# A two-layer hybrid block on one core: the high parts of the weight tiles are cast on GpSimd instead of ScalarE during attention

## The chip, the cores and the metric

The kernel runs on one core of one Trainium2 chip. The metric is the time of one execution on the device in microseconds, as the median of several runs. The engines are TensorE (PE in the rows, PEld its weight loads), VectorE (DVE), ScalarE (ACT), GpSimd (POOL) and SyncE (SP), which here issues the DMAs.

## The reference

Two layers work on 512 latent tokens and 256 context tokens of width 1024. In each, a modulated RMS norm feeds one wide projection, whose columns go to three mixers (windowed attention with a sink and rotary positions, multi-scale pooling, a Fourier mix) and three gates. The branches are gated, summed and projected; a gated MLP with a depthwise convolution follows.

```python
h = modulate(rms_norm(x, norm_mix[l]), sh1, sc1)
k, v, q, u, f, gt = jnp.split(h @ w_in[l], IN_SPLITS, axis=-1)
q = apply_rope(q.reshape(B, T, N_Q_HEADS, HEAD_DIM), cos, sin)
o = latent_attention(q, k, v, kc, vc, attn_sink[l])
y = (g_a * (o_attn @ w_br_attn)
     + g_p * (multiscale_pool(pool_in, pool_w, pool_scale) @ w_br_pool)
     + g_f * (fourier_mix(four_in) @ w_br_four))
x = x + g1 * (y @ w_out)
x = x + g2 * conv_ffn(hf, w_up[l], conv_w[l], w_down[l])
```

In layer 0 the context tokens go the same way (768 columns in all); in layer 1 only their keys and values are needed, and 512 columns run through the rest.

## The kernel before

Activations lie with channels on the partitions and tokens along the columns. The large products are made in float32r with every operand split into a high part (the value rounded to float32r) and a low part (the rest): a product is three matmuls, high by high, high by low and low by high (`mmk`, line 373). The split of a weight tile is made on the chip, in `halves` (line 345): a cast of the raw tile on ScalarE writes the high part `whi` (line 353), and VectorE subtracts it from the raw tile to get the low part `wlo` (line 354). A tile is 128 partitions by 1024 columns. There are three buffers each for the raw tile, for `whi` and for `wlo`.

Tiles are drawn in a planned order (`_plan`, line 70). `weights` (line 362) hands out the tile at the head, after `ahead` (line 357) has loaded and split the one behind it; so each draw splits the next tile. The raw tiles are loaded by DMAs from SyncE's queue (`raw`, line 340).

The attention phase (`attention`, line 753) lays two kinds of work side by side on TensorE. One is the attention proper, in units of one head pair and one block of 128 queries: `scores` makes the scores in PSUM (lines 688 to 699; there is one such PSUM buffer), VectorE takes the maximum (line 704) and the bias (line 707), ScalarE the exponentials (lines 713 and 715), VectorE the sums and the scaling (lines 716 to 720); `turn_p` transposes the result on TensorE (line 736) and copies it out (line 737), one unit later; `pv` multiplies by the values (line 747), two units later. The other kind stands in the list `BESIDE`: four query tiles (`q_steps`, line 637) and eight gates of the Fourier branch (`gate_steps`, line 598), cut into steps that are put between the units. A query tile draws one `w_in` tile, and a gate draws one, with a `w_brf` tile before every fourth gate. Behind a query tile's matmuls stands its rope: a copy out of PSUM (line 628), a shuffle on VectorE (line 631), one product on VectorE (line 632) and one on GpSimd (line 633), their sum (line 634), the cast and the subtraction into the query tiles (lines 647 and 648). A gate ends with tanh on ScalarE (line 607), a product on VectorE (line 613) and a sum on GpSimd (line 615).

The order on TensorE in this phase is the program's own (`manual_schedule`, line 892). On the other engines a planner orders the instructions when the program is built, by its own estimate of when each one becomes ready; so an instruction that goes to another engine, or takes another time there, may also change the order of its neighbours. Each engine then works through its queue in order.

Of the kernel before, what the change touches and what calls it, by code (L numbers as in the profile page):

```python
# [69 lines left out]
def _plan(l):  # L70
    tiles = lambda *ms: [("w_in", l, m) for m in ms]

    def gates(name, first, n):
        for m in range(8):
            if m % n == 0:
                yield (name, l, m // n)
            yield ("w_in", l, first + m)

    yield from tiles(0, 1, 4, 5, 2, 3) if l else tiles(3)
    yield from gates("w_brp", 10, 4)  # L80
    if l == 0:
        yield from tiles(4, 5)
    gf = gates("w_brf", 18, 4)
    for kind, j in BESIDE:
        if kind == "q":
            yield ("w_in", l, 6 + j)
        else:
            yield from (next(gf) for _ in range(1 + (j % 4 == 0)))
    for m in range(8):
        if m % 2 == 0:  # L90
            yield ("w_bra", l, m // 2)
        yield ("w_in", l, 26 + m)
    for ms in (range(8), range(KEEP[0])):
        yield from (("w_out", l, m) for m in ms)
    for c, (j0, n) in enumerate(FF_CHUNKS):
        for j in range(j0, j0 + n):
            yield from (("w_up", l, j), ("w_up", l, NFF + j))
        if 0 < c < len(FF_CHUNKS) - 1:
            yield from (("w_dn4", l, c - 1, i) for i in range(4))
    for ms in (range(8), range(0 if l else KEEP[0])):  # L100
        yield from (("w_dn6", l, m) for m in ms)


class Lazy:
    def __init__(self, make, n):
        self.make, self.t = make, [None] * n
# [33 lines left out]
class Kern:  # L140
    def __init__(self, ctx, tc, a):
        self.tc, self.nc, self.a = tc, tc.nc, a
        e = ctx.enter_context
        self.cp = e(tc.tile_pool(name="cp", bufs=1))
        self.wr = e(tc.tile_pool(name="wr", bufs=3))
        self.wp = e(tc.tile_pool(name="wp", bufs=3))
        self.sm = e(tc.tile_pool(name="sm", bufs=4))
        self.dp = e(tc.tile_pool(name="dp", bufs=1, space=bass.MemoryType.DRAM))
        self.sp = e(tc.tile_pool(name="sp", bufs=NSLOT))
        self.mm_pool = e(tc.tile_pool(name="mp", bufs=NP, space=bass.MemoryType.PSUM))  # L150
        self.cv_pool = e(tc.tile_pool(name="cv", bufs=2))
        self.tg_pool = e(tc.tile_pool(name="tg", bufs=1))
        self.scopes, self.nph, self.turn, self.cturn = [], 0, 0, 0
        self.fill = iter(())
        self.plan = deque(k for l in range(NL) for k in _plan(l))
        self.ready = deque()
        self.pend = iter(())
# [187 lines left out]
    def halves(self, raw, eng=None, stay=False):  # L345
        nc = self.nc
        n = raw.shape[-1]
        if stay:
            hi, lo = self.slot(), self.slot()
        else:  # L350
            hi = self.wp.tile([P, 1024], F32R, tag="whi", name="whi")[:, 0:n]
            lo = self.wp.tile([P, 1024], F32R, tag="wlo", name="wlo")[:, 0:n]
        self.cpy = nc.scalar.copy(hi, raw)  # L353
        (eng or nc.vector).tensor_tensor(lo, raw, hi.bitcast(F32), ALU.subtract)  # L354
        return hi, lo

# [434 lines left out]
    def layer(self, l, xs, streams, h=None, after=None):  # L791
        nc, a = self.nc, self.a
# [96 lines left out]
        ka, kb, vs = kv if l else self.attn_kv(l, hs, ls, both)  # L889
        self.phase(dict(sc=1, tp=2, tv=1), SBB)  # L890
        o = self.slots(4, F32)
        with self.tc.manual_schedule(engines={mybir.EngineType.PE}):
            self.attention(l, ka, kb, vs, o, hs, ls, fhi, flo, y, streams, ncol // P)
        self.phase(dict(mm=6 - NP, aux=2), SBA)
        ohi, olo = self.slots(4), self.slots(4)
        for t in range(4):
# [348 lines left out]
```

## Time and profile before

| what | us |
|---|---|
| median of 3 runs (1844.81 to 1847.6) | 1847.33 |
| the profiled execution | 1845.27 |
| span of the profiled execution, first to last instruction | 1843.5 |
| TensorE busy in the span | 1813.4 |
| VectorE busy | 1185.3 |
| ScalarE busy | 661.9 |
| GpSimd busy | 95.0 |

The attention phase of layer 0 lies at about 188 to 380 us of the span, that of layer 1 at about 1209 to 1350 us. Busy time on TensorE is read with care: matmuls are pipelined and their ends are modelled, so what matters is where TensorE has an idle stretch before an instruction and who released it. A wait for several semaphores is put down to the one that came last.

### The profile page before, as it was taken

Reading aid. Unit: us, or ns where it says so; the run is one execution under the profiler, and the core shown is the slowest. Engines: PE = TensorE matmul, PEld = TensorE weight load, DVE = VectorE, ACT = ScalarE, POOL = GpSimd, SP = SyncE. Lnnn points to the kernel's source line nnn. Section 1 sums busy time; section 2 is a strip of 40 time slices with the busy share of each in tenths; the row PEclk is TensorE's granted clock in tenths of the full one; section 3 lists DMA queues with packets and bytes.
Section 4 is the critical chain, followed back from the end, with each engine's and each line's share of the span. In section 5 each row is a group of like instructions: output and inputs, shape, how many; then the busy total and the mean of one; then the engine's idle time right before and its main releaser. Section 6 shows DMA issues by size and latency. Waiting matters only on the chain.

```text
span 1843.5 us, 26717 instructions
## 1 busy us (share of the span) xinstructions
PE 1813.4 (98%) x10592; PEld 1563.6 (85%) x10592; DVE 1185.3 (64%) x2244; ACT 661.9 (36%) x1121; POOL 95.0 (5%) x74
## 2 busy tenths in 40 slices
PE   7999999999999999999999999999999999999997
PEld 5888888888898888888888898878788988888887
DVE  4777666667759985757566567556644675556555
ACT  4322544422234331323232244344533453333323
POOL 1000111112000000000000000011121000000000
PEclk9999999999999999999999999999999999999999
DMA  9345101134542442424233343321123523233222
GB/s 347 119 122 159 58 29 53 35 100 138 173 128 92 149 126 80 130 77 135 83 123 95 98 145 121 99 79 36 63 83 106 172 92 103 92 103 92 95 86 72
DMA packets 74701, 197.60 MB, mean 107 GB/s; under 512 B 8145, under 2 KB 15569, under 8 KB 74449
## 3 DMA queue, kind: packets, MB, share of 16 engines
q1 hardware_dynamic: 74576, 195.90, 33.7%
q8 instruction: 83, 1.36, 0.3%
q14 instruction: 42, 0.34, 0.1%
HBM read 191.68 MB, written 4.19 MB: 106 GB/s over the span
## 4 chain that ended last, share of the span: by engine, by line
PE 93%; ACT 2%; DVE 2%; issue 1%; DMA 1%; POOL 0%; SPq 0%; DVEq 0%; ACTq 0%; POOLq 0%
PE mm L378 50%; PE mp L378 34%; PE tv L747 2%; PE tp L736 1%; ACT p L713 1%; PE sc L688 1%; PE aux L552 0%; PE aux L568 0%; PE aux L415 0%; ACT whi L353 0%; PE sc L689 0%; PE sc L691 0%; PE sc L692 0%; DMA slot<-in_w_m_dram 0%; PE aux L286 0%
## 5 line engine op out<-in xcount | busy, mean ns | idle before, releaser
L378 PE MATMUL mm<-slot,whi 128*128 128x512 f32 (+1 forms) x3308 | 861.0, 349 | 4.6 <-ACT slot L444 3.8
L378 PEld LDWEIGHTS mm<-slot,whi 128*128 128x128 f32 x3308 | 580.2, 190 | 86.0 <-ACT slot L444 4.2
L378 PE MATMUL mp<-slot,whi 128*128 128x512 f32 (+1 forms) x2360 | 620.1, 351 | 3.4 <-ACT tg L607 3.2
L378 PE MATMUL mm<-slot,wlo 128*128 128x512 f32 (+1 forms) x1654 | 575.5, 348 | 0.0
L378 PEld LDWEIGHTS mp<-slot,whi 128*128 128x128 f32 x2360 | 410.5, 189 | 67.1 <-issue 7.5
L354 DVE TENSOR_TENSOR wlo<-wraw,whi 128x1024 fp32r<-128x1024 f32 (+1 forms) x242 | 295.4, 1222 | 230.2 <-ACT whi L353 224.2
L353 ACT CAST whi<-wraw 128x1024 fp32r<-128x1024 f32 (+1 forms) x243 | 251.6, 1038 | 525.3 <-PE mm L378 303.5
L378 PE MATMUL mp<-slot,wlo 128*128 128x512 f32 (+1 forms) x1180 | 410.7, 348 | 0.0
L378 PEld LDWEIGHTS mm<-slot,wlo 128*128 128x128 f32 x1654 | 313.2, 189 | 40.2 <-DVE wlo L354 0.8
L378 PEld LDWEIGHTS mp<-slot,wlo 128*128 128x128 f32 x1180 | 223.3, 189 | 29.6 <-DVE wlo L354 0.8
L320 DVE SCALAR_TENSOR_TENSOR junk<-wmod,cb 128x512 f32<-128x512 f32 x256 | 177.5, 693 | 7.6 <-DMA wmod<-in_w_mt_dram 4.1
L1051 DVE SCALAR_TENSOR_TENSOR slot<-mm,mod,slot 128x512 f32<-128x512 f32 (+1 forms) x86 | 54.7, 638 | 65.1 <-PE mm L378 64.9
L971 DVE SCALAR_TENSOR_TENSOR cp<-mm,p,cp 128x511 f32<-128x511 f32 (+2 forms) x122 | 79.1, 650 | 20.2 <-ACT cp L970 18.4
L615 POOL TENSOR_TENSOR slot<-slot,tg 128x512 f32<-128x512 f32 (+1 forms) x45 | 61.0, 1355 | 344.9 <-DVE tg L613 289.7
L418 POOL TENSOR_TENSOR sm<-sm,p 128x2 f32<-128x2 f32 (+1 forms) x10 | 10.8, 1083 | 1081.2 <-DVE sm L417 1081.2
L704 DVE TENSOR_REDUCE sm<-sc 128x2 f32<-128x1024 f32 (+2 forms) x40 | 48.8, 1221 | 25.2 <-PE sc L699 17.9
L713 ACT ACTIVATE p<-sc,sm 128x512 f32<-128x512 f32 (+2 forms) x80 | 54.4, 686 | 10.6 <-DVE sm L707 10.4
L970 ACT ACTIVATE cp<-mm,p 128x512 f32<-128x512 f32 (+1 forms) x60 | 36.8, 613 | 59.1 <-PE mm L378 57.7
L400 ACT ACTIVATE st<-slot 128x256 f32<-128x256 f32 (+1 forms) x70 | 32.3, 478 | 48.9 <-DVE slot L1051 22.1
L1051 DVE SCALAR_TENSOR_TENSOR slot<-mp,mod,slot 128x512 f32<-128x512 f32 (+1 forms) x42 | 26.2, 623 | 35.9 <-PE mp L378 35.8
L971 DVE SCALAR_TENSOR_TENSOR cp<-mp,p,cp 128x511 f32<-128x511 f32 (+2 forms) x62 | 38.0, 617 | 14.0 <-ACT cp L970 13.1
L747 PE MATMUL tv<-pt,slot 128*64 128x128 f32 x640 | 43.9, 279 | 0.3 <-ACT pt L737 0.3
(182 smaller groups left out, 1392.0 us busy)
## 6 DMA issues: line engine op xcount, KB each, us to landing
wraw<-in_w_up_dram SPq DMA_DIRECT2D x88, 512.0 KB, 3.5
wmod<-in_w_mt_dram SPq DMA_DIRECT2D x160, 256.0 KB, 3.1
wraw<-in_w_in_dram SPq DMA_DIRECT2D x68, 512.0 KB, 3.5
wraw<-in_w_dn_dram SPq DMA_DIRECT2D x32, 512.0 KB, 3.5
wraw<-in_w_out_dram SPq DMA_DIRECT2D x26, 512.0 KB, 3.6
wraw<-in_w_dn_dram SPq DMA_DIRECT2D x21, 384.0 KB, 3.2
slot<-in_w_m_dram SPq DMA_DIRECT2D x20, 384.0 KB, 7.7
wraw<-in_w_bra_dram SPq DMA_DIRECT2D x8, 512.0 KB, 3.5
```

The costliest lines, as they stand in the source:

```text
L320: nc.vector.scalar_tensor_tensor(junk[:, 0:512], w, 1.0, self.cb[:, b, hs], ALU.mult, ALU.mult, accum_out=acc[:, b * 2 + h : b * 2 + h + 1])
L353: self.cpy = nc.scalar.copy(hi, raw)
L354: (eng or nc.vector).tensor_tensor(lo, raw, hi.bitcast(F32), ALU.subtract)
L378: self.mm = self.nc.tensor.matmul(out, ww, xx, start=(k == 0 and i == 0), stop=(k == n - 1 and i == 2))
L400: nc.scalar.activation(sq, xs[k][:, c0:c1], AF.Square)
L615: eng.tensor_tensor(y[:, c0 : c1], y[:, c0 : c1], tg[:, c0:c1], ALU.add)
L704: nc.vector.tensor_reduce(mx, both, AX.X, ALU.max)
L713: nc.scalar.activation(p[:, :w], ps[h], AF.Exp, bias=ngm[:, h : h + 1], scale=0.125, accum_out=den[:, h : h + 1])
L747: nc.tensor.matmul(po[64 * h : 64 * h + 64, :], vs[:, c * P + 64 * h : c * P + 64 * h + 64], pt[:, i * P : (i + 1) * P], start=(j == 0), s ...
L970: nc.scalar.activation(c[:, c0:c1], ps, AF.Copy, scale=cw(1))
L971: tap = lambda d, src, i: nc.vector.scalar_tensor_tensor(c[:, d], src, cw(i), c[:, d], ALU.mult, ALU.add)
L1051: self.nc.vector.scalar_tensor_tensor(xv, ps, g2(m, b), xv, ALU.mult, ALU.add)
```

## The change

A flag, `pool_hi`, is set around the attention phase of each layer. While it is set, `halves` makes the high part with a copy on GpSimd instead of the one on ScalarE. The low part is made on VectorE as before, and everything outside the phase stays as it was.

```diff
@@ -151,7 +151,7 @@
-        self.fill = iter(())
+        self.fill, self.pool_hi = iter(()), False
@@ -350,7 +350,10 @@
-        self.cpy = nc.scalar.copy(hi, raw)
+        if self.pool_hi:
+            nc.gpsimd.tensor_copy(hi, raw)
+        else:
+            self.cpy = nc.scalar.copy(hi, raw)
         (eng or nc.vector).tensor_tensor(lo, raw, hi.bitcast(F32), ALU.subtract)
@@ -889,8 +892,10 @@
         o = self.slots(4, F32)
+        self.pool_hi = True
         with self.tc.manual_schedule(engines={mybir.EngineType.PE}):
             self.attention(l, ka, kb, vs, o, hs, ls, fhi, flo, y, streams, ncol // P)
+        self.pool_hi = False
```

## Rows read from the trace of the kernel before

**Rows 1.** The page, busy us, share of the span, instructions of each engine.

```profile
PE 1813.4 (98%) x10592; PEld 1563.6 (85%) x10592; DVE 1185.3 (64%) x2244; ACT 661.9 (36%) x1121; POOL 95.0 (5%) x74
```

**Rows 2.** Windows: stretch, its us, each engine's busy us, clock, DMA.

```profile
188.50:379.00 190.50, 188.23 (x1396) 161.80 (x1397) 120.12 (x249) 87.22 (x219) 23.65 (x19) 1.00 0.13 41
1209.00:1350.00 141.00, 136.30 (x938) 111.90 (x937) 94.66 (x178) 69.33 (x159) 18.52 (x11) 0.99 0.18 56
```

**Rows 3.** Timeline, TensorE: start, us, instruction, idle before it and releaser.

```profile
254.90 0.72 PE L378 MATMUL mp<-slot,whi 128*128 128x512 f32 x2 [0.41 <-ACT tg L607]
...
1222.21 0.39 PE L688 MATMUL sc<-slot 128*128 128x256 f32 x1 [0.69 <-DVE slot L648]
...
1245.02 0.73 PE L378 MATMUL mp<-slot,whi 128*128 128x512 f32 x2 [1.95 <-ACT tg L607]
...
1284.44 0.39 PE L688 MATMUL sc<-slot 128*128 128x256 f32 x1 [0.73 <-ACT p L713]
...
1306.33 0.39 PE L688 MATMUL sc<-slot 128*128 128x256 f32 x1 [1.03 <-ACT p L713]
```

**Rows 4.** Windows, the 5 us behind the longest wait.

```profile
1245.00:1250.00 5.00, 4.98 (x29) 4.38 (x31) 3.66 (x7) 0.65 (x2) 1.28 (x1) 0.66 0.39 105
```

**Rows 5.** The page, groups: the casts, busy us and mean ns, idle before.

```profile
L353 ACT CAST whi<-wraw 128x1024 fp32r<-128x1024 f32 (+1 forms) x243 | 251.6, 1038 | 525.3 <-PE mm L378 303.5
```

**Rows 6.** Timeline, ScalarE, layer 1's attention stretch.

```profile
1215.21 1.05 ACT L353 CAST whi<-wraw 128x1024 fp32r<-128x1024 f32 x1 [4.32 <-PE mp L378]
...
1216.17 0.58 ACT L628 COPY cp<-mp 128x512 f32<-128x512 f32 x1
...
1242.72 0.80 ACT L713 ACTIVATE p<-sc,sm 128x640 f32<-128x640 f32 x1
...
1275.28 1.08 ACT L353 CAST whi<-wraw 128x1024 fp32r<-128x1024 f32 x1
...
1297.88 1.05 ACT L353 CAST whi<-wraw 128x1024 fp32r<-128x1024 f32 x1 [0.79 <-PE mp L378]
...
1298.83 0.57 ACT L628 COPY cp<-mp 128x512 f32<-128x512 f32 x1
```

**Rows 7.** Timeline, VectorE, layer 1's attention stretch.

```profile
1216.30 1.22 DVE L354 TENSOR_TENSOR wlo<-wraw,whi 128x1024 fp32r<-128x1024 f32 x1 [3.84 <-ACT whi L353]
...
1242.53 0.16 DVE L707 SCALAR_TENSOR_TENSOR sm<-sm,nsink 128x2 f32<-128x2 f32 x1
...
1277.00 1.21 DVE L354 TENSOR_TENSOR wlo<-wraw,whi 128x1024 fp32r<-128x1024 f32 x1
...
1278.12 1.76 DVE L632 TENSOR_TENSOR cp<-cp,p 128x512 f32<-128x512 f32 x1
...
1298.96 1.23 DVE L354 TENSOR_TENSOR wlo<-wraw,whi 128x1024 fp32r<-128x1024 f32 x1 [0.42 <-ACT whi L353]
```

**Rows 8.** Timeline, GpSimd, two-input products and the subtraction.

```profile
21.83 3.12 POOL L354 TENSOR_TENSOR wlo<-wraw,whi 128x1024 fp32r<-128x1024 f32 x1 [7.49 <-ACT whi L353]
...
203.54 1.29 POOL L615 TENSOR_TENSOR slot<-slot,tg 128x512 f32<-128x512 f32 x1 [7.24 <-DVE tg L613]
...
295.16 0.73 POOL L615 TENSOR_TENSOR slot<-slot,tg 128x256 f32<-128x256 f32 x1 [10.46 <-DVE sm L709]
```

**Rows 9.** Waits in 185 to 346 and 1205 to 1350: us, times, longest.

```profile
DVE wlo L354 <- ACT whi L353: 7.9, 5, 3.2
...
DVE wlo L354 <- ACT whi L353: 10.7, 6, 5.0
```

**Rows 10.** Timeline, GpSimd and VectorE where they overlap.

```profile
209.32 0.73 DVE L709 TENSOR_TENSOR sm<-sm,nsink 128x2 f32<-128x2 f32 x1
...
1277.25 2.09 POOL L633 TENSOR_TENSOR cp<-cp,p 128x512 f32<-128x512 f32 x1 [13.08 <-DVE cp L631]
...
1289.66 1.30 POOL L615 TENSOR_TENSOR slot<-slot,tg 128x512 f32<-128x512 f32 x1 [10.33 <-DVE tg L613]
...
1289.75 2.29 DVE L354 TENSOR_TENSOR wlo<-wraw,whi 128x1024 fp32r<-128x1024 f32 x1 [0.17 <-ACT whi L353]
```

## What the time was predicted to be, and from what

> **What bounds the kernel now.** The first view to read is the page's busy times: TensorE is busy 98% of the span, GpSimd 5% [rows 1]. A change that moves work between two other engines can therefore only give back time in which TensorE stands still, or make it stand still more. So the second view is the busy time of the two attention stretches, one per layer [rows 2]: TensorE is busy 188.23 of 190.50 us in layer 0 and 136.30 of 141.00 us in layer 1. It idles 2.27 + 4.70 = 6.97 us there, 0.38% of the span. The third view, TensorE's timeline, tells where [rows 3]: in layer 0 there are small waits, of which 0.41 us is one of the largest; in layer 1 0.69, 1.95, 0.73 and 1.03 us carry most. After the 1.95 us the granted clock is 0.66 for 5 us [rows 4], between the levels of 1.2 and 2.4 GHz, which costs another 5 x 0.34 = 1.7 us. So 6.97 + 1.70 = 8.7 us is all that the change can win, in both layers together.
>
> **What moves.** In each layer twelve `w_in` tiles and two `w_brf` tiles are drawn in the attention phase, and each draw casts the next tile: 14 casts a layer, 28 in all. One takes 1038 ns on average on ScalarE [rows 5], 1.05 at most places, so ScalarE loses 28 x 1.05 = 29.4 us, and GpSimd, which now runs 30 instructions for 23.65 + 18.52 = 42.2 us there [rows 2], gets as many longer. No DMA moves: the weight loads stay on SyncE's queue. VectorE's subtraction (line 354) stays too, but waits for GpSimd in place of ScalarE.
>
> **What the removal gives.** ScalarE is not short of time, so only casts that stand in front of something late count. I looked, for each of the larger TensorE waits, at what ScalarE and VectorE did before it.
> - Wait of 0.69 us at 1222.21. It ends the rope chain of the first query tile: copy out of PSUM (line 628), shuffle, GpSimd's multiply, add, cast, subtraction. The cast at 1215.21 waits for TensorE to release its buffer, and the copy, which needs the end of the same tile, starts only at 1216.17: 0.96 us lost [rows 6]. Then line 354 stands in front of the shuffle on VectorE as well [rows 7].
> - Wait of 1.03 us at 1306.33: the same picture, cast at 1297.88, copy at 1298.83, line 354 at 1298.96 [rows 6, 7].
> - Wait of 0.73 us at 1284.44: the cast at 1275.28 brings line 354 to 1277.00, ahead of the rope product at 1278.12 [rows 6, 7].
> - Wait of 1.95 us at 1245.02, the largest: a cast stands right ahead of the exponential that starts at 1242.72, but the bias for it is made by line 707 at 1242.53 + 0.16 = 1242.69 [rows 6, 7]. The cast costs 0.03 us there. I count nothing.
> The bound is 0.69 + 1.03 + 0.73 = 2.45 us, and nothing is lost by a removal alone. I take the first two in full and half of the third, where the subtraction and not the cast is in the way: 2.1 us. What is late next is the rest of the same chain, VectorE and GpSimd.
>
> **What the cast costs on GpSimd.** No row shows a one-input GpSimd instruction of this size. Its two-input product of 512 columns takes 1.29 us and of 256 columns 0.73 [rows 8], so 2.19 ns a column and 0.17 fixed: 1024 columns would take 2.4 us, and the one subtraction of that size, with the same output type, took 3.12 [rows 8]. ScalarE's 1.05 is the other end. One operand in place of two would halve the slope: 0.17 + 1.12 = 1.3 us, which I take, as it is the nearer of the two sizes to a plain copy; both ends, 1.05 and 2.4, go into the range. The Trainium skill, GPSIMD Engine Reference, section Engine selection, calls GpSimd's one-input instructions roughly line-rate; at its 1.2 GHz that makes an estimate of 0.85 us plus start, about 1.02 with 0.17, and no row here shows it. By that price the next term would vanish.
>
> The waits. VectorE stands 7.9 + 10.7 = 18.6 us in 11 waits for the cast before line 354 [rows 9]. A cast of 1.3 makes each 0.25 longer, one of 2.4 makes each 1.35 longer. TensorE sees it at the three rope places above: 0.75 us, at most 4.05. On GpSimd itself the cast takes ScalarE's wait for a buffer with it. Behind it stand the gate sums (line 615), whose result is wanted by nobody before the next gate's 24 matmuls are through, and the rope product (line 633). That one needs the copy and the shuffle first, which take longer together than 1.3 us, so a cast released by the same matmul is over by then. The tiles themselves are in time: TensorE waits for none of them in either stretch.
>
> The shared port. When GpSimd and VectorE work on SBUF together, one stands still: VectorE's product at 1278.12 took 1.76 beside a GpSimd product that itself took 2.09, and its subtraction at 1289.75 took 2.29 (1.22 elsewhere) beside one at 1289.66 [rows 7, 10]. I found nine such stretched VectorE instructions in the two stretches, the first at 209.32 and the last at 1289.75 [rows 10], together 6.4 us over their usual times, for 30 GpSimd instructions. TensorE felt 0.73 (at 1284.44) and 0.41 (at 254.90) of it [rows 3], 1.14 us. For 28 more instructions of 1.3 us against a mean of 42.2 / 30 = 1.41: 1.14 x 28/30 x 1.3/1.41 = 1.0 us. The bounds: nothing, and with 2.4 us a cast and every VectorE delay felt 6.4 x 28/30 x 2.4/1.41 = 10.2 us. The Trainium skill has a rule that speaks against this change (SBUF — State Buffer, section Who interferes with whom): VectorE instructions with two SBUF inputs, or in a mode that uses two ports, share a port pair with GpSimd, the first takes it for its whole length and the other blocks. The trace agrees: the excess of the subtraction, 1.07 us, is no longer than the GpSimd instruction beside it, 1.30 [rows 10]. By the rule alone, with the softmax scaling (line 720) and the subtractions as its victims, the time would be that of the second rival.
>
> The sum: -2.1 + 0.75 + 1.0 = -0.35 us. The profiled execution took 1845.27 us, so 1844.9; the median of the three runs, 1847.33, is 2.06 above it, which makes 1847.0.
>
> **The rivals.** (1) Clearly faster. If the rope chains get shorter by more than the waits behind them, and the 1.95 us wait shrinks enough that the clock stays at 2.4 GHz, 2.45 + 1.95 + 1.70 - 1.0 = 5.1 us go: 1842.2. For it: that wait's chain begins with a rope too, and the planner that orders VectorE's and GpSimd's queues is free to put line 354 later. Against it: the exponential waits for VectorE there, not for the cast. (2) Slower, by the port. If a cast takes 2.4 us on GpSimd and lands on line 720 or on the query subtractions, half of the 10.2 us is felt, 5.1, plus 4.05 by later subtractions, less 2.1: +7.0, 1854.3. For it: VectorE is busy 67% of layer 1's stretch [rows 2] and the softmax runs over it. Against: TensorE felt a sixth of such delays so far. It decides from about 2 us a cast, where loss passes gain by the 0.2%. (3) Slower, by GpSimd's order: a cast is put right before a rope product that is ready. Eight ropes, of which six are needed soon, 6 x 1.3 = 7.8 us less 2.1: 1853. Against: a cast is ready well before. (4) The casts lie in idle time on either engine and nothing moves: 1847.3, inside the forecast.
>
> **How the numbers follow.** A measurement of this kernel can tell about 0.2%, 3.7 us, from no change. Forecast with rival 4: 0.57, with its own range of 1843.6 to 1851. Rival 1: 0.21. Rival 2: 0.17, rival 3: 0.05. So faster 0.21, same 0.57, slower 0.22, and the time is the forecast's, 1847.0. The range takes in rival 1 and nearly rival 2: 1842 to 1854.
>
> **What would show it.** Right: 28 casts of about 1.3 us on GpSimd in the attention stretches, 28 fewer on ScalarE; the waits at the first and third rope of layer 1 under half; line 720's longest times above 1.2 us more often; TensorE's idle time in the two stretches 6 to 8 us in all. Wrong: casts of over 2 us, TensorE waits for line 720 or 648, a second stretch of low clock (slower); or a full clock through layer 1 and under 3 us idle (faster).

## The result, and the profile after

The changed kernel takes 1858.68 us (median of 6 runs, 1856.26 to 1860.9), the kernel before 1845.6 (6 runs beside it): a ratio of 1.0069, 95% interval 1.0056 to 1.0082. That is slower by 13 us, outside the range that was predicted.

The page, busy times (the answer to [rows 1]):

```profile
PE 1815.9 (98%) x10592; PEld 1564.6 (84%) x10592; DVE 1200.2 (65%) x2244; ACT 636.1 (34%) x1093; POOL 124.1 (7%) x102
```

28 instructions have gone from ScalarE to GpSimd, and nothing else has changed in number. TensorE's busy time is 2.5 us longer and its span 12.7: it stands still for longer. The windows of the two attention stretches say where (the answer to [rows 2]; the stretches begin and end a little later now), and the third row is ten microseconds of layer 1:

```profile
190.00:383.00 193.00, 188.82 (x1395) 161.82 (x1394) 124.09 (x251) 74.84 (x206) 37.87 (x31) 1.00 0.13 42
1213.50:1361.00 147.50, 135.16 (x927) 110.59 (x927) 102.92 (x177) 55.70 (x143) 32.44 (x25) 0.99 0.17 53
1310.00:1320.00 10.00, 7.34 (x51) 6.10 (x50) 6.34 (x15) 5.65 (x16) 0.00 (x0) 0.83 0.10 27
```

TensorE runs the same 10,592 instructions in the same order in both kernels, so each can be set beside its counterpart. By that the profiled execution lost 2.2 us in its first 60 us, 2.5 in layer 0's attention, 8.4 in layer 1's, and between them and behind them nothing over 0.3. The first 60 us are chance: a run of the kernel before, unchanged, differed there by 1.3 us from the first one. In the stretches TensorE's idle time went from 2.27 to 4.18 and from 4.70 to 12.34 us. The low clock behind the 1.95 us wait [rows 4] is gone, and the one at 1310 (0.83 over 10 us) has come in its place.

What it waits for, from TensorE's waits (us in total, times, longest), of before first, then of after:

```profile
PE sc L688 <- ACT p L713: 2.2, 3, 1.0
PE tv L736 <- DVE p L720: 0.6, 2, 0.3
```

```profile
PE tv L739 <- DVE p L723: 8.2, 6, 2.5
PE sc L691 <- ACT p L716: 3.1, 2, 2.7
PE tp L739 <- DVE p L723: 2.2, 3, 1.3
```

From line 353 on, a line of before has its number raised by three: line 723 is the softmax scaling (720 before), 739 the transposes that need it (736), 357 the subtraction (354), 354 now the cast on GpSimd. In the rows of the experiments the numbers shift again; the tiles tell which it is: `wlo<-wraw,whi` the subtraction, `p<-p,sm` the scaling, `sm<-sm,sm` the sums, `tv` and `tp` the transposes. The waits for the scaling were 0.6 us and are 10.4 us. These two rows alone hold most of the loss. So the scaling comes too late, and it is VectorE's queue that must be read. First the casts (GpSimd's groups) and VectorE's waits for them:

```profile
L354 POOL CAST whi<-wraw 128x1024 fp32r<-128x1024 f32 x28 | 30.2, 1077 | 210.6 <-issue 120.7 <-PE mm L381 77.3 <-PE mp L381 11.9
...
DVE wlo L357 <- POOL whi L354: 22.0, 11, 5.0
```

A cast is no slower on GpSimd, 1077 ns on average against 1038 on ScalarE [rows 5], and VectorE's waits for these casts have grown from 18.6 us in 11 [rows 9] to 22.0 us in 11. The cast is shorter than was predicted, and the waits grew by about as much as was predicted (0.31 us each, for 0.25). What changed is where the waits stand. Here is the worst place, on GpSimd, VectorE and TensorE:

```profile
1277.96 1.04 POOL L354 CAST whi<-wraw 128x1024 fp32r<-128x1024 f32 x1 [10.04 <-issue]
1281.07 1.76 POOL L636 TENSOR_TENSOR cp<-cp,p 128x512 f32<-128x512 f32 x1 [2.07 <-DVE sm L721]
...
1277.28 0.16 DVE L712 TENSOR_TENSOR sm<-sm,nsink 128x2 f32<-128x2 f32 x1
1279.03 1.23 DVE L357 TENSOR_TENSOR wlo<-wraw,whi 128x1024 fp32r<-128x1024 f32 x1 [1.59 <-POOL whi L354]
1280.17 0.15 DVE L719 TENSOR_TENSOR sm<-sm,sm 128x2 f32<-128x2 f32 x1
1280.25 0.73 DVE L634 STREAM_SHUFFLE cp<-cp 128x512 f32<-128x512 f32 x1
1280.88 0.15 DVE L721 RECIPROCAL sm<-sm 128x2 f32<-128x2 f32 x1
1281.02 0.69 DVE L635 TENSOR_TENSOR cp<-cp,p 128x512 f32<-128x512 f32 x1
1281.63 2.02 DVE L723 TENSOR_SCALAR p<-p,sm 128x640 f32<-128x640 f32 x2
...
1283.79 0.41 PE L739 MATMUL tv<-p,p 128*128 128x128 f32 x2 [2.53 <-DVE p L723]
```

The same softmax in the kernel before, on VectorE:

```profile
1274.96 0.16 DVE L716 TENSOR_TENSOR sm<-sm,sm 128x2 f32<-128x2 f32 x1 [1.73 <-ACT sm L715]
1275.15 0.17 DVE L718 RECIPROCAL sm<-sm 128x2 f32<-128x2 f32 x1
1275.43 1.02 DVE L720 TENSOR_SCALAR p<-p,sm 128x640 f32<-128x640 f32 x2
1276.37 0.74 DVE L631 STREAM_SHUFFLE cp<-cp 128x512 f32<-128x512 f32 x1
```

There the subtraction stood behind the scaling and the shuffle, at 1277.00 [rows 7]. Now it stands between the last small step behind the bias (L712) and the sums (L719), and waits 1.59 us for a cast that began at 1277.96. The queue is worked through in order, so the sums, the reciprocal and the scaling wait with it, and two rope operations have slipped in as well. The scaling then takes 2.02 us for the 1.02 of before, with a GpSimd product beside it. Of the 80 scalings 10 now take over 0.7 us, where 3 did; 8 of the 10 stand beside a product or gate sum that GpSimd had before, and 2 beside a cast. In the kernel before, 7 of the 28 subtractions stand inside a softmax in this way; in the changed one 13.

TensorE now has seven long idle times in the stretches (1.77 us at 310.70; 0.87, 1.04, 2.53, 2.66, 1.64 and 1.34 in layer 1, the last with 0.69 close behind it), together 12.5 us; the kernel before had 1.03 us in all at the same instructions. At three of them, 5.2 us, the subtraction waits inside the softmax for a cast just begun: the one above, one at 1252.56, and this:

```profile
1336.32 1.23 DVE L357 TENSOR_TENSOR wlo<-wraw,whi 128x1024 fp32r<-128x1024 f32 x1 [2.07 <-POOL whi L354]
1338.33 2.06 DVE L723 TENSOR_SCALAR p<-p,sm 128x640 f32<-128x640 f32 x2
...
1340.53 0.41 PE L739 MATMUL tv<-p,p 128*128 128x128 f32 x2 [1.64 <-DVE p L723]
```

At three of the others (310.70, 1243.45, 1354.92) it stands ahead of the scaling without such a wait, and VectorE is blocked beside GpSimd. At 1243.45 it stood there in the kernel before as well (1233.35 there); new is the rope behind it, ahead of the scaling, with a product that takes 1.78 us beside GpSimd's:

```profile
1239.69 1.78 DVE L635 TENSOR_TENSOR cp<-cp,p 128x512 f32<-128x512 f32 x1
```

At 310.70 the tiny sums, 0.15 us elsewhere, take 1.01 beside the cast, and the subtraction still comes before the scaling:

```profile
307.21 1.04 POOL L354 CAST whi<-wraw 128x1024 fp32r<-128x1024 f32 x1 [2.71 <-issue]
...
307.25 1.01 DVE L719 TENSOR_TENSOR sm<-sm,sm 128x2 f32<-128x2 f32 x1 [1.15 <-ACT sm L718]
308.40 1.22 DVE L357 TENSOR_TENSOR wlo<-wraw,whi 128x1024 fp32r<-128x1024 f32 x1
309.55 1.01 DVE L723 TENSOR_SCALAR p<-p,sm 128x640 f32<-128x640 f32 x2
```

The 2.66 us at 1314.05 is one of the three rope places where a gain was expected (1306.33 before [rows 3]):

```profile
1303.89 1.05 POOL L354 CAST whi<-wraw 128x1024 fp32r<-128x1024 f32 x1 [6.95 <-issue]
1306.03 2.16 POOL L636 TENSOR_TENSOR cp<-cp,p 128x512 f32<-128x512 f32 x1 [1.08 <-DVE cp L634]
...
1303.49 1.80 DVE L723 TENSOR_SCALAR p<-p,sm 128x640 f32<-128x640 f32 x2
1306.97 1.77 DVE L635 TENSOR_TENSOR cp<-cp,p 128x512 f32<-128x512 f32 x1
...
1310.78 1.26 ACT L650 CAST slot<-cp 64x512 fp32r<-64x512 f32 x2 [3.43 <-DVE cp L637]
1312.34 0.79 ACT L716 ACTIVATE p<-sc,sm 128x640 f32<-128x640 f32 x1
...
1314.05 0.58 PE L691 MATMUL sc<-slot 128*128 128x256 f32 x1 [2.66 <-ACT p L716]
```

The scaling (beside the cast) and the rope product (beside GpSimd's) are stretched, and on ScalarE the first exponential now stands behind the rope's cast; in the kernel before it stood ahead of it.

### The profile page after: what moved, and what is told of

Its sections match the earlier page's. It is cut to its first block, busy times and chain, and to the rows that moved or that the text cites. A ratio compares the mean times of both kernels' runs of the same rounds, so it can differ in the third digit from the quotient of the medians.

```text
span 1856.2 us, 26714 instructions
## 1 busy us (share of the span) xinstructions
PE 1815.9 (98%) x10592; PEld 1564.6 (84%) x10592; DVE 1200.2 (65%) x2244; ACT 636.1 (34%) x1093; POOL 124.1 (7%) x102
## 4 chain that ended last, share of the span: by engine, by line
PE 89%; DVE 3%; issue 3%; DMA 2%; ACT 2%; SPq 0%; POOL 0%; DVEq 0%; ACTq 0%
PE mm L381 50%; PE mp L381 33%; PE tv L750 2%; PE tp L739 1%; DMA slot<-in_w_m_dram 1%; ACT p L716 1%; DVE p L723 1%; PE aux L555 0%; PE aux L571 0%; PE sc L691 0%; DVE wlo L357 0%; PE aux L418 0%; DMA wraw<-in_w_in_dram 0%; DVE sm L707 0%; PE sc L692 0%
## 5 line engine op out<-in xcount | busy, mean ns | idle before, releaser
L356 ACT CAST whi<-wraw 128x1024 fp32r<-128x1024 f32 (+1 forms) x215 | 222.2, 1036 | 505.1 <-PE mm L381 299.0
L723 DVE TENSOR_SCALAR p<-p,sm 128x512 f32<-128x512 f32 (+2 forms) x80 | 43.8, 589 | 2.2
```

Of the source, the lines that this page charges most:

```text
L723: nc.vector.tensor_scalar(pr[h][:, :w], pr[h][:, :w], rc[:, h : h + 1], None, ALU.mult)
```

## The experiments

All times below are ratios to the kernel before on the same chip, with their 95% intervals; "stretches" are layer 0's and layer 1's attention in the profile, in us against before.

**Is it chance?** The kernel before, unchanged:

> The kernel before, unchanged, once more under a name of its own. Its first 60 us, before anything that the change touches, took 2.2 us longer in the profile of the changed kernel and between 0.7 less and 3.7 more in four others. If that is chance from run to run, this run differs from the kernel before by nothing in the median and by some us in its own first 60 us; the stretches behind that agree within 0.3 us.

1.0001 (0.9992 to 1.0010); stretches 0.0 and 0.0, first 60 us -1.3. The changed kernel once more:

> The changed kernel once more, nothing edited. Its two stretches of attention were 10.9 us longer than before in the profile, its medians 13.1 us. If the loss is that of the stretches and the first 60 us vary by chance, 1856 to 1859 us, and its stretches again 10 to 12 us longer with the same long stalls of TensorE for the softmax scaling; if the loss was partly chance, under 1855 us.

1.0068 (1.0055 to 1.0081), 1858.62 us; stretches +2.5 and +11.5, TensorE's idle time in them the same to 0.01 us. So layer 1's loss varies by 3 us between two executions, idle time hardly, and the first 60 us by chance. The 3 us are the clock's (this run's windows):

```profile
1310.00:1320.00 10.00, 7.34 (x44) 6.24 (x43) 5.67 (x14) 5.67 (x16) 0.00 (x0) 0.66 0.08 26
1355.00:1365.00 10.00, 8.86 (x60) 6.92 (x61) 2.80 (x4) 1.74 (x4) 1.43 (x1) 0.83 0.20 67
```

The first run had 0.83 and 1.00 in these two windows, so by an estimate 10 x 0.17 + 10 x 0.17 = 3.4 us more were lost by the lower clock, behind the same waits.

The change in layer 0 alone (`self.pool_hi = l == 0`):

> The change in layer 0 alone. Nothing is left out. By the alignment of the two traces the stretch of layer 0 costs 2.5 us and that of layer 1 8.4 us; so 1847 to 1849 us, and the rest comes with layer 1. Order: ten subtractions inside a softmax instead of thirteen. Port: layer 0 has half of the casts, and so half of the loss, 6 us: 1851 to 1853.

1.0007 (0.9998 to 1.0016); stretches +2.5 and 0.0. Most of the loss is layer 1's.

**Is it the shared port?** The kernel before, with 28 copies more on GpSimd, of the raw tile onto itself behind its subtraction:

```diff
         (eng or nc.vector).tensor_tensor(lo, raw, hi.bitcast(F32), ALU.subtract)
+        if self.pool_hi:
+            nc.gpsimd.tensor_copy(raw, raw)
```

> The kernel before, cast on ScalarE, with 28 GpSimd copies added in the attention phases: each copies a raw tile of 128x1024 onto itself behind the subtraction, and only the raw buffer's release waits for it. Nothing is left out. The subtractions stand where they stood before (7 inside a softmax). Port: 28 instructions of about 1.04 us that read and write SBUF next to VectorE's scalings cost what the casts cost, 8 us or more: 1853 or more. Order: the port alone costs little, 0 to 3 us: 1845 to 1849.

1.0013 (1.0004 to 1.0022); stretches +0.2 and +1.9. The copies take 1.13 us each, as much as the casts, and cost some 2 us. VectorE's order is that of the kernel before, instruction by instruction. Traffic of that size alone, a little later than the casts', is not the cause.

**The subtraction on GpSimd too**, in the changed kernel:

```diff
+        if self.pool_hi:
+            eng = nc.gpsimd
         (eng or nc.vector).tensor_tensor(lo, raw, hi.bitcast(F32), ALU.subtract)
```

> The changed kernel, with the subtraction of the same 28 tiles on GpSimd too. Nothing is left out. VectorE has no subtraction of weight tiles in the attention phases, and GpSimd is busy by 28 x (1.04 + 2.4 to 3.1) us. Order: with no subtraction left in VectorE's queue the loss goes, 1845 to 1850 us. Port: GpSimd holds the port three times as long, so the loss grows past the changed kernel's: 1862 us or more.

1.0142 (1.0126 to 1.0157), the slowest; stretches +14.3 and +12.3. VectorE has no weight subtraction in the way any more, but 19 of the 80 scalings take over 0.7 us (3 in the kernel before, 10 in the changed one), and TensorE's waits for them are 16.0 us. GpSimd takes 2.46 us on average for a subtraction; beside those, VectorE is blocked for longer than beside a cast.

**The order held.** The subtraction is put behind the last scaling that the program has written before it, so that none stands inside a softmax; on the changed kernel, and on the kernel before as a control:

```diff
+        with self.after(*self.scaled):
             (eng or nc.vector).tensor_tensor(lo, raw, hi.bitcast(F32), ALU.subtract)
...
+            sc_i = nc.vector.tensor_scalar(pr[h][:, :w], pr[h][:, :w], rc[:, h : h + 1], None, ALU.mult)
+        self.scaled = (sc_i,)
```

> The changed kernel, with one more edge: on VectorE the low-part subtraction of a tile drawn in the attention phase is queued behind the last softmax scaling traced before it (order only, no wait). Nothing is left out. Two theories. Order: the cast on GpSimd is done while ScalarE still makes the exponentials, so the planner puts the subtraction, which waits for the cast and takes 1.2 us, between the softmax bias and the softmax scaling (13 of 28 in the changed program, 7 before), and TensorE's transposes wait for the scaling. Then holding it back gives nearly all of the loss behind the start phase back: 1845 to 1849 us, TensorE's waits for the scaling under 2 us in sum (10.4 us in the changed kernel's trace). Port: the loss is GpSimd's casts and sums locking VectorE out (scalings of 2.0 us for two 0.5 us). The casts stay where they are, so at least two thirds of the loss stay: 1854 us or more.

> The kernel before, cast on ScalarE, with the same order edge on the subtraction. Nothing is left out. Order: seven subtractions that stood inside a softmax move behind it; 1842 to 1846 us, a little faster than before or the same. Port: no GpSimd instruction is added, so the same as before, 1844 to 1847. With the first run it makes a square (cast on ScalarE or GpSimd, subtraction free or held): order expects a large effect of the edge under the GpSimd cast alone, port expects the GpSimd cast to cost 8 us or more with and without the edge.

1.0086 (1.0072 to 1.0100) and 1.0091 (1.0077 to 1.0105): both slow, and alike, so the edge itself does it. In each layer one tile's subtraction is held back until TensorE stands waiting for it (TensorE's timeline, changed kernel with the edge):

```profile
316.90 0.79 PE L383 MATMUL mp<-slot,wlo 128*128 128x512 f32 x1 [6.10 <-DVE wlo L359]
```

It is the tile split at the draw of a `w_brf` tile, which is wanted at once. The same two kernels without the edge for that one:

```diff
+        kept_sc = self.scaled
+        if key[0] == "w_brf":
+            self.scaled = ()
```

> The changed kernel with the order edge of the first experiment (the subtraction of a tile drawn in the attention phase is queued on VectorE behind the last softmax scaling traced before it), save for the one tile a draw of w_brf splits, which is wanted at once and whose subtraction came 6 us late there. Nothing is left out. Order: with no other cost of the edge, the attention stretches take what they took before, within 2 us each, and the whole 1844 to 1849 us, with all 28 casts on GpSimd. Port: the casts on GpSimd still cost most of the 13 us, 1853 or more.

> The kernel before, cast on ScalarE, with the same edge and the same exception. Nothing is left out. Order: seven subtractions leave the softmax, 1842 to 1846 us; if the order in the kernel before already costs nothing, equal to it. It gives the comparison for the run with the cast on GpSimd: the difference of the two is what the move costs with the order held.

1.0012 (1.0003 to 1.0020) with the casts on GpSimd, 1.0004 (0.9995 to 1.0013) with them on ScalarE. With the same edge in both (VectorE's orders then differ in some eight instructions of 2244), the move costs 0.08%, 1.2 us by the medians, which these intervals do not tell from nothing; by the stretches of the two profiles (+2.6 and -0.25 against +1.4 and -1.8) it costs 2.8 us. So 11 of the 13 us are in the order. They are layer 1's: layer 0's 2.5 us are still there with the casts on GpSimd.

**Position, or the wait for a late cast?** The subtraction of each tile is put inside the next unit's softmax, where its cast is long done (a tile drawn before that gets its subtraction at the draw); first with the casts on ScalarE, then on GpSimd:

```diff
-        (eng or nc.vector).tensor_tensor(lo, raw, hi.bitcast(F32), ALU.subtract)
+        low = lambda: (eng or nc.vector).tensor_tensor(lo, raw, hi.bitcast(F32), ALU.subtract)
+        if self.pool_hi:
+            self.late.append((hi, low))
...
-        nc.vector.tensor_tensor(es, ngm, sk, ALU.subtract)
+        bias = nc.vector.tensor_tensor(es, ngm, sk, ALU.subtract)
...
+        with self.after(bias):
+            lows = [t[1]() for t in self.late]
+        self.late = []
+        with self.after(*lows):
+            nc.vector.tensor_tensor(den, den, es, ALU.add)
```

> The casts stay on ScalarE, as in the kernel before, but the subtraction of each weight tile is placed on VectorE inside the next unit's softmax, between the masked bias and the row sums, in 23 of 28 cases (7 in the kernel before, 13 in the changed one). Its cast is long done by then, so VectorE does not wait for it there. Theory A, the position alone costs (1.23 us of subtraction ahead of each scaling, 16 softmaxes more than before): 11 us or more, so 1857 us or later. Theory B, it is the wait for a late cast and the scaling beside a GpSimd operation that cost, and a subtraction that is ready fits into the time in which VectorE waits for the exponentials: 1845 to 1849 us.

> As the run before it, with the casts on GpSimd: 24 of 28 subtractions inside a softmax, each long after its cast. Theory B (the wait for the late cast): 1845 to 1850 us, with the 1 to 2 us that the shared port was seen to cost. Theory A (the position) or a larger cost of the port: 1857 us or later. If the run with ScalarE is near 1846 and this one is near 1858, the cost is the port's.

1.0054 (1.0042 to 1.0067) and 1.0083 (1.0070 to 1.0097). By the time alone this would speak for the position. TensorE's waits say otherwise (casts on ScalarE):

```profile
PE mp L386 <- DVE wlo L355: 9.4, 4, 3.3
...
PE tv L748 <- DVE p L732: 1.5, 3, 0.9
```

With 23 of 28 subtractions inside a softmax, TensorE waits 1.5 us for scalings. The 9.4 us are four waits for the low part itself, two at the start of each layer, where a tile is wanted within the same unit; the same fault as in the first attempt to hold the order. So the same again, with the first four tiles of a layer left as they were:

```diff
-        if self.pool_hi:
+        self.nth += 1
+        if self.pool_hi and self.nth > 4:
             self.late.append((hi, low))
```

> As the run with the casts on ScalarE and each subtraction inside the next unit's softmax, but the first four tiles of each layer, two of which TensorE had waited for there (9.4 us in four waits, and the lower clock behind one of them), have their subtraction at once. 19 subtractions are left inside a softmax (13 in the changed kernel). Theory A, the position alone costs: 1855 us or later, and TensorE waits for the scaling of the softmax as long as in the changed kernel, about 10 us. Theory B, a subtraction that is ready fits there: 1845 to 1849 us, and these waits are 1 to 3 us.

> As the run before it, with the casts on GpSimd: 20 subtractions inside a softmax, each one unit behind its cast. The changed kernel's cast, port traffic and number of tiles are kept, and more subtractions than its 13 stand inside a softmax, but none has to wait there for a cast that has just begun. Theory B (the wait for a late cast): 1846 to 1852 us, the upper end if the port costs more beside the scalings than the 2 us seen with spare copies. If the position with the port is what costs: 1857 us or later.

1.0004 (0.9995 to 1.0013) on ScalarE and 1.0011 (1.0001 to 1.0020) on GpSimd; stretches +1.0 and -1.8, and +2.4 and +0.6. The last one has all 28 casts on GpSimd and 20 subtractions inside a softmax, more than the changed kernel's 13, and 11 of the 13 us are gone, again in layer 1. VectorE there, at a softmax of layer 1:

```profile
1267.99 1.22 DVE L358 TENSOR_TENSOR wlo<-wraw,whi 128x1024 fp32r<-128x1024 f32 x1
1269.70 0.16 DVE L732 TENSOR_TENSOR sm<-sm,sm 128x2 f32<-128x2 f32 x1 [0.48 <-ACT sm L727]
1270.10 1.01 DVE L736 TENSOR_SCALAR p<-p,sm 128x640 f32<-128x640 f32 x2
```

The subtraction starts without a wait; when it is done VectorE still waits 0.48 us for the exponentials. It lies in time that was idle. The same sums in the kernel before:

```profile
1267.84 0.16 DVE L716 TENSOR_TENSOR sm<-sm,sm 128x2 f32<-128x2 f32 x1 [1.62 <-ACT sm L715]
```

TensorE's waits for scalings in the run with all the casts on GpSimd and ready subtractions:

```profile
PE tv L752 <- DVE p L736: 2.8, 4, 1.8
PE tp L752 <- DVE p L736: 2.8, 2, 2.6
```

5.6 us, of which the two longest, 1.8 and 2.6, are what is left of the seven places: sums blocked beside a cast (layer 0's, 1.77 us at 310.70 of the changed kernel), and the last tile, whose subtraction still waits 1.83 us for its cast. The other five are gone.

**The new order without the move.** The same order in layer 1 alone, casts on ScalarE (`self.pool_hi, self.nth = l == 1, 0`):

> As the run with early casts on ScalarE and the first four tiles of a layer left out, but only in layer 1; layer 0 is as in the kernel before. In that run layer 1's stretch was 1.8 us shorter than before and layer 0's 1.0 us longer. If both are the order's doing: 1844 us, 0.1% under the kernel before, at the edge of what the comparison can tell. If the 1.8 us are a matter of that profile: 1845 to 1847 us.

0.9988 (0.9979 to 0.9997), 1844.23 us against 1846.12; stretches 0.0 and -3.3, idle time in layer 1 3.33 us (4.70 before). A gain of 0.1%, at the edge of what the comparison can tell, by the place of the subtraction alone. Of the 3.3 us, 1.4 are idle time; 1.7 are that the granted clock stayed at 1.00 behind a wait of 1.96 us, where it fell to 0.66 for 5 us behind the 1.95 of before [rows 4]. The two waits are as good as equal, so this part may be chance:

```profile
1247.34 0.73 PE L387 MATMUL mp<-slot,whi 128*128 128x512 f32 x2 [1.96 <-ACT tg L616]
...
1245.00:1250.00 5.00, 3.04 (x22) 2.44 (x21) 4.29 (x10) 2.59 (x8) 1.00 (x1) 1.00 0.27 105
1250.00:1255.00 5.00, 5.00 (x39) 4.10 (x38) 3.87 (x9) 2.35 (x8) 0.28 (x1) 1.00 0.23 80
```

## Why the prediction was wrong

- **What bounds the kernel** was right: the loss is in the two stretches, and nearly all of it is TensorE's idle time there, 6.97 us before and 16.5 after, 9.5 of the 10.9 us that the profiled stretches lost.
- **The cast's price** was taken too high, not too low: 1.04 us at most places for the 1.3 taken. Half the slope of a two-input row was the wrong neighbour for it; ScalarE's own row was the nearer one. The Trainium skill calls one-input instructions roughly line-rate (GPSIMD Engine Reference, section Engine selection), and the trace agrees: the estimate by it was 1.02, and the cast took 1.04.
- **The shared port** was small, as predicted, if not as small: 1.0 us was predicted; some 2 were lost with spare copies, and in the two pairs with nearly one order and the casts on either engine 1.2 and 0.7 by the medians, within their noise, and 2.8 and 3.7 by the stretches of one profile each. VectorE is seen to block beside GpSimd at nearly full length in the sums of 1.01 us, with two inputs of two columns each, beside a cast of 1.04. The Trainium skill says that a VectorE instruction with two SBUF inputs contends with a GpSimd instruction that reads SBUF (SBUF — State Buffer, section Who interferes with whom); the trace agrees, by these two rows.
- **The removal** did not give its -2.1 us at the three rope waits: 0.69 became 0.86, 0.73 went, and 1.03 became 2.66. The longest wait, 1.95, which I counted at nothing, fell to 0.71. (The 0.73 stands in the sum twice, half of it as a gain here and the whole as a delay by the port.) With ready subtractions the four are, in the order 0.69, 0.73, 1.03 and 1.95 of before, 0.85, 0, 0.08 and 0.71 with the casts on GpSimd, but 0.69, 0, 0.39 and 1.92 with the casts still on ScalarE. So of the 2.8 us less, 1.4 are the order's. The removal gives the other 1.4, nearly all of it (1.2) at the wait counted at nothing, and none at the first rope. That one is the longest of TensorE's waits for tanh (line 607), here with the casts on ScalarE, then on GpSimd:

```profile
PE mp L387 <- ACT tg L616: 3.2, 4, 1.9
PE mp L390 <- ACT tg L619: 2.2, 4, 0.7
```

- **The step that failed is the waits, 0.75 us.** It kept the subtractions where they stood and made each wait longer by 0.25; the waits did grow by about that, 3.4 / 11 = 0.31 each, but by luck: the 0.25 was to come from a cast of 1.3 us, and the cast took 1.04. What failed is where they stand. The planner moved six more subtractions into softmaxes, and some of them wait there for a cast just begun. The text said that the planner orders the queues and used it only as a hope for the faster rival. Its price was not bounded: the upper end of 4.05 us was for the old places. In its place stand 12.5 us at seven instructions of TensorE: 5.2 at the three waits for a late cast inside a softmax, and 7.3 at four places where VectorE's scalings, sums or rope product are stretched beside a GpSimd instruction.
- **The level.** The 2.06 us added to get from the profiled execution to the median were chance: over six runs the median of before is 1845.6, beside 1845.27.
- **The rivals.** The sign named for the second, TensorE waiting for line 720, is what came; its mechanism, a cast of over 2 us, did not (1.04 at most places). The third had an order go wrong, on GpSimd in place of VectorE. None had it on VectorE.

What stays open: the share of the port in the loss of the changed kernel. Ready subtractions took away 11 of 13 us with all the casts left on GpSimd; but four of the seven places show blocked VectorE instructions rather than the wait, and two of these went with the new order too. Layer 0's 2.5 us went with neither order (+2.6 with the edge, +2.4 with ready subtractions), so the order is shown as the cause for layer 1 alone. Why the planner put the subtraction there is only argued: with the cast gone from ScalarE's queue it may count on an earlier end of the cast. What the cast itself waited for on GpSimd, the profile tells for few: for 6 of the 28 it names TensorE, for 20 nobody.

## What to carry to other kernels

Moving an instruction to an idle engine moves its consumers in the queues of other engines, when a planner orders them: ask which queue the consumer stands in, what stands behind it, and price the case that it is put one critical step earlier. A wait total per engine says little here (18.6 us and 22.0); what counts is whether the wait lies ahead of something that the bounding engine needs. An instruction that is ready can lie in another chain's idle time at no cost that the times here tell (1.0004), and an experiment that shifts one must leave out the few tiles that are wanted at once.

## What the hardware showed unexpectedly

A cast of 128x1024 from fp32 to fp32r takes 1.04 us on GpSimd at most places, as on ScalarE, while the two-input subtraction of that size takes 2.46 on average (29 of them, with both on GpSimd). A VectorE operation on 128x2 elements, 0.15 us, can be held up for nearly a whole GpSimd cast, 1.01 us.
